# The last norm of all rows read before the last three experts' sums, their tokens' rows summed and written apart

## The chip, the cores and the metric

The kernel runs on one core of a Trainium2 chip. What counts is the time of one execution on the device in microseconds (us). A core has five engines, each with an instruction queue of its own that it works off in order: TensorE (PE, with its weight loads as PEld), VectorE (DVE), ScalarE (ACT), GpSimd (POOL) and SyncE (SP). SyncE only issues transfers here; GpSimd issues the indirect ones, which gather or scatter rows by a list of row numbers. HBM is the chip's main memory, SBUF the core's working memory of 128 partitions, PSUM the memory that TensorE writes its sums to.

## The reference

One decoder layer over 2048 tokens of 1024 numbers: a mixer of attention and a gated recurrence, then a mixture of 32 experts, of which each token takes two, then a last norm. Only the end bears on the change:

```python
x = x + mixed @ w_out[layer]
h2 = rmsnorm(x, norm2_g[layer])
x = x + hier_moe(h2, ...)      # each token: two experts, silu(h @ w_gate) * (h @ w_up) @ w_down, times a gate
...
return rmsnorm(x, norm_f_g)    # x * rsqrt(mean(x * x) + 1e-6) * g, row by row
```

A row of the output depends on that row's sum alone: the residual x and the two experts' rows of the token. Most rows are therefore complete before the last expert has run.

## The kernel before

The layer ends in `phase_c` (L1567), a loop over 32 experts sorted by their number of tokens; each has a fixed capacity of rows (`CAPS`: 192 down to 128). `even_order` (L101) decides in which order they run: the first is fixed, the others are mixed so that large and small ones alternate, and the last two are held back for the end. The experts are called E0 to E31 here, by their place in that order. The last ones have these capacities: E26 188, E27 128, E28 128, E29 192, E30 128, E31 128. A large expert (over 128) takes TensorE longer in each stage, and its result has to be transposed back and is scattered in two pieces, of 128 rows and of the rest.

For each expert there is a gather of its tokens' rows of h2 (`expert_in`, L1679, GpSimd), transposes (`expert_x`), the products with gate and up weights (`expert_up`), the hidden transposes of a small expert (`expert_hid`, L1756), the down product (`expert_down`, L1767) and the scatter of the result, which adds the rows onto the tensor x2d in HBM (`expert_out`, L1806, an accumulating indirect transfer on GpSimd). Each scatter into x2d waits for the landing of the one before, since both may touch one row. TensorE's program order is written out by hand: up of E(r), then down of E(r-1), and so on; the last is up of E30, down of E29, down of E30, up of E31, down of E31. The result transposes of a large expert E(r) stand in the up stage of E(r+2), or, for E29, in the down stage of E30. Weights come through SyncE: eight pieces of 0.5 MB for gate and up, four for down (`weights_down`, L1673, tile eD, eight buffers, so the four of an expert wait until the expert two places ahead has used its own).

The end, before the change, is this. While E31's up stage runs, nothing else is moved but the last scatters. Once E30's rows are scattered into x2d, `expert_base` (L1834) gathers E31's token rows from x2d into a tile, and `final` (L1851) loads all 16 tiles of 128 rows of x2d, forms each row's sum of squares on ScalarE (L1843), the reciprocal root in seven small steps of ScalarE and VectorE (`rsqrt`, L182), multiplies on VectorE (L1849) and stores the tile into the output. E31's down product is never added to x2d: VectorE adds it to the gathered rows (L1794), these are normed the same way, and when all 16 stores have landed one indirect scatter writes them over the output's rows (L1811). A list entry that is no token has a row number beyond the output and is skipped there. After that, `overflow` (L1420) runs only if an expert had more tokens than its capacity.

SyncE's transfers to and from one tensor and buffer are held apart by semaphores, and each transfer on SyncE waits for the one eight places ahead of it to have landed.

## Time and profile before

| | us |
|---|---|
| median of 3 runs | 2217.72 (2206.78 to 2219.48) |
| the profiled execution | 2217.23 |
| its span | 2215.3 |
| TensorE busy | 1967.0 (89%) |
| VectorE busy | 1493.8 (67%) |
| ScalarE busy | 1201.4 (54%) |
| GpSimd busy | 567.3 (26%) |
| transfers of SyncE's queue, share of 16 engines | 56.7% |
| transfers of GpSimd's queue, share of 16 engines | 8.5% |

The profile is of one execution, taken by the hardware. The span runs from its first to its last instruction, and all points of time below are counted from its start. "Busy" adds up an engine's instructions; an average over stages with different limits says little on the end, so the rows further down are of the last 160 us. A wait is put down to what ended it last.

### The profile page before, as it was taken

What the parts mean: (1) busy time and instruction counts of PE and PEld (TensorE: products, weight loads), DVE (VectorE), ACT (ScalarE), POOL (GpSimd) and SP (SyncE); (2) the same over time, 40 slices, a digit from 0 to 9 for tenths busy, and PEclk for the clock granted to TensorE, in tenths of its full rate; (3) what the DMA queues carried; (4) which work ended last, traced back from release to release, by engine and by line L of the source; (5) the groups of instructions that cost most, each with busy time, mean ns of one, the idle gap of its engine ahead of it and who ended that gap; (6) DMA issues with size and microseconds to landing.
All of it is one profiled execution on the core that took longest, in us unless ns stands there. A gap on an engine that the chain in (4) does not pass through costs nothing. (4 is left out here: it accounts for less than half of the span.)

```text
span 2215.3 us, 39749 instructions
## 1 busy us (share of the span) xinstructions
PE 1967.0 (89%) x13753; PEld 1345.8 (61%) x13777; DVE 1493.8 (67%) x4121; ACT 1201.4 (54%) x2646; POOL 567.3 (26%) x620
## 2 busy tenths in 40 slices
PE   4998978999899998899888998699999999999981
PEld 4645565555655556455444445569999977766750
DVE  6657787767857777567887677756656656556525
ACT  6455653765547655566554343456556655555524
POOL 2303244123431335411431112212233222111110
PEclk9998988998999998999899998799999999999995
DMA  7333254532535324553578995799999999999857
GB/s 229 85 94 96 66 128 112 114 90 70 118 101 123 83 75 113 174 119 71 128 168 226 290 253 164 253 353 315 312 311 314 329 315 313 325 325 321 302 149 299
DMA packets 438896, 433.37 MB, mean 196 GB/s; under 512 B 242644, under 2 KB 325716, under 8 KB 438176
## 3 DMA queue, kind: packets, MB, share of 16 engines
q1 hardware_dynamic: 420464, 382.74, 56.7%
q0 software_dynamic: 14064, 46.46, 8.5%
q8 instruction: 109, 1.79, 0.3%
q10 hardware_dynamic: 4160, 1.58, 0.3%
q14 instruction: 99, 0.81, 0.1%
HBM read 305.30 MB, written 66.29 MB: 168 GB/s over the span
## 5 line engine op out<-in xcount | busy, mean ns | idle before, releaser
L1660 DVE TENSOR_TENSOR eL<-eraw,eH 128x1024 bf16<-128x1024 f32 x248 | 298.0, 1218 | 107.9 <-ACT eH L1654 97.0
L1654 ACT ACTIVATE eH<-eraw 128x1024 fp32r<-128x1024 f32 x252 | 258.4, 1053 | 123.8 <-PE acc L1745 48.8
L453 ACT ACTIVATE P<-S,orow,fqk 128x256 f32<-128x256 f32 (+1 forms) x384 | 195.0, 512 | 172.3 <-DVE orow L447 94.1
L567 PE MATMUL proj<-whh,x 128*128 128x512 f16 x512 | 202.4, 395 | 0.1
L568 PE MATMUL proj<-whl,x 128*128 128x512 f16 x512 | 200.1, 391 | 0.0
L569 PE MATMUL proj<-whh,x 128*128 128x512 f16 x512 | 199.5, 390 | 0.0
L1726 PE MATMUL acc<-xs,eH 128*128 128x352 f32 (+15 forms) x1216 | 195.2, 313 | 1.8 <-DVE xs L1704 1.8
L436 PE MATMUL S<-k,qs 128*128 128x256 f16 (+1 forms) x768 | 172.4, 355 | 13.9 <-ACT P L453 10.9
L1726 PEld LDWEIGHTS acc<-xs,eH 128*128 128x128 f32 x1216 | 176.2, 190 | 4.7 <-issue 2.2
L440 DVE CUSTOM_DVE_ANT_0 S<-S,bias 128x256 f32<-128x256 f32 (+1 forms) x384 | 141.4, 369 | 54.8 <-PE S L436 51.6
L456 DVE TENSOR_TENSOR Ps<-P,Ps 128x256 f16<-128x256 f32 (+1 forms) x192 | 129.7, 675 | 68.8 <-ACT Ps L455 67.2
L1828 POOL DMA_INDIRECT x2d<-yo,sidx x49 | 105.2, 2146 | 255.7 <-DVE yo L1803 95.8
L1776 PE MATMUL acc<-hs,eD 128*128 128x176 f32 (+15 forms) x1216 | 165.1, 295 | 4.9 <-DVE ts L1751 3.0
L1776 PEld LDWEIGHTS acc<-hs,eD 128*128 128x128 f32 x1216 | 161.1, 190 | 6.0 <-DVE ts L1751 3.9
L1687 POOL DMA_INDIRECT xg<-h2d,gidx x49 | 56.1, 1146 | 334.0 <-PE tr L1701 159.6
L436 PEld LDWEIGHTS <-qs 128*128 128x128 f16 x768 | 89.5, 123 | 69.3 <-issue 20.3
L260 POOL TENSOR_TENSOR wraw<-wraw,g 128x1024 f32<-128x1024 f32 x44 | 84.7, 1928 | 167.8 <-DMA wraw<-in_w_in_dram 134.5
L1744 PE MATMUL acc<-eH,xs 128*128 128x512 f32 x208 | 118.4, 569 | 0.0
L1788 PE MATMUL acc<-eD,hs 128*128 128x512 f32 x208 | 98.0, 609 | 21.2 <-ACT yo L1801 11.5
L386 PE MATMUL proj<-wh,x 128*128 128x128 f16 x512 | 96.5, 231 | 18.9 <-DVE V L394 18.9
L455 ACT ACTIVATE Ps<-P 128x256 f16<-128x256 f32 (+1 forms) x192 | 102.8, 536 | 7.6 <-DMA PT<-Ps 5.0
L658 POOL TENSOR_SCALAR sw<-Sp,hw 128x128 f32<-128x128 f32 x112 | 53.3, 476 | 196.5 <-DVE Sp L661 106.5
(396 smaller groups left out, 4891.6 us busy)
## 6 DMA issues: line engine op xcount, KB each, us to landing
eraw<-in_w_gate_dram SPq DMA_DIRECT2D x128, 512.0 KB, 7.1
eD<-in_w_down_dram SPq DMA_DIRECT2D x128, 512.0 KB, 6.4
eraw<-in_w_up_dram SPq DMA_DIRECT2D x124, 512.0 KB, 6.3
wraw<-in_w_in_dram SPq DMA_DIRECT2D x41, 512.0 KB, 4.1
od<-orow SPq DMA_DIRECT2D x64, 132.0 KB, 2.0
R<-od SPq DMA_DIRECT2D x64, 132.0 KB, 2.4
xt<-in_x_dram SPq DMA_DIRECT2D x16, 512.0 KB, 4.8
wraw<-in_w_out_dram SPq DMA_DIRECT2D x16, 512.0 KB, 4.1
```

Of the source, the lines that this page charges most:

```text
L436: nc.tensor.matmul(ps[:, h, :W], q, self.block_cols(D['k'][h][:, x], br, blk, True), start=(x == 0), stop=(x == 1))
L440: nc.vector.tensor_tensor_reduce(ps[:, h, :W], ps[:, h, :W], bias[:, 256 - W:256], 1.0, -3.0e38, OP.add, OP.max, mx[:, h:h + 1])
L453: nc.scalar.activation(P[:, h], ps[:, h, :W], AF.Exp, bias=nm[:, h:h + 1], scale=f[:, h:h + 1], accum_out=orow[:, 130 + h:131 + h])
L456: nc.vector.tensor_tensor(hv[:, 1], P, hv[:, 0], op=OP.subtract)
L567: nc.tensor.matmul(ps, self.XH[n // 4][:, k, ns], W['whh'][:, k, :], start=(k == 0), stop=False)
L568: nc.tensor.matmul(ps, self.XH[n // 4][:, k, ns], W['whl'][:, k, :], start=False, stop=False)
L569: nc.tensor.matmul(ps, self.XL[n // 4][:, k, ns], W['whh'][:, k, :], start=False, stop=(k == KT - 1))
L1654: nc.scalar.activation(H, raw, AF.Copy)
L1660: (nc.gpsimd if on_pool else nc.vector).tensor_sub(L, raw, H.bitcast(F32))
L1726: nc.tensor.matmul(gu[:, i, 0:2 * cap], w[:, o:o + 128], xs[:, k], start=(k == 0), stop=False, skip_group_check=True)
L1744: nc.tensor.matmul(gu[:, j], xs[:, k, 0], H[:, fs], start=(k == 0), stop=False)
L1776: nc.tensor.matmul(py[:, j, 0:cap], W['w_down', f][:, o:o + 128], hs[:, f], start=(f == 0), stop=(f == 3))
```

## The change

The order holds back three experts instead of two (`LATE`), so the 192 one becomes E28, and E29, E30 and E31 are all of capacity 128. The last norm of all rows starts from x2d as it is when E28's rows are in it, while E30's down stage and E31's stages run. The rows of E29, E30 and E31 no longer go into x2d. Instead `late_base` gathers the token rows of the three from x2d and writes them into the tensor mix (whose old content is no longer needed); E29's and E30's results are added onto mix by accumulating scatters; `late_rows` gathers the three experts' rows from mix; E31's result is added to its own tile of these on VectorE, as before. `late_out` norms the three tiles and scatters them into the output, one after the other, behind all stores. `final` is split into loads, norms and stores of some tiles (`final_load`, `final_norm`, `final_store`), with one chain of small steps for a group of tiles instead of one for each; the tiles lie in the buffers eraw, eH and eD. The rest of the diff are the overflow code's bounds.

```diff
-NB = NE + 1
+NB = NE + LATE            # LATE = 3
@@ even_order
-    last = left[-2:]
-    left = left[:-2]
+    last = left[-LATE:]
+    left = left[:-LATE]
@@ phase_c
+                    if r == NE - 2:
+
+                        self.late_base()
+                        self.final_load(0, RAW)
+                        self.weights_down(E[r + 1])
+                        self.final_load(RAW, 9)
                     if r == NE - 1:
-                        self.expert_base(E[r])
-                        self.final()
+                        for e in (E[r], E[r - 1], E[r - 2]):
+                            self.late_rows(e)
...
+                    if r == NE - 1:
+                        self.final_norm(RAW, 9)
+                        self.final_store(3, 9)
+                        self.final_load(13, NT)
                     if r >= NE - 2:
                         for _ in self.expert_down(E[r]):
                             next(out, None)
-                        out = chain(out, self.expert_out(E[r]))
+                        if r < NE - 1:
+                            out = chain(out, self.expert_out(E[r]))
+                    if r == NE - 2:
+                        self.final_norm(0, RAW)
+                        self.final_store(0, 3)
+                        self.final_load(9, 13)
...
-                    if r + 1 < NE:
+                    if r + 1 < NE - 1:
                         self.weights_down(E[r + 1])
-                for _ in out:
-                    pass
+                self.final_norm(9, 13)
+                self.final_store(9, 13)
+                self.final_norm(13, NT)
+                self.final_store(13, NT)
+                for e in E[-LATE:]:
+                    self.late_out(e)
@@ expert_out
-            nc.gpsimd.indirect_dma_start(out=self.x2, in_=yo, in_offset=None,
+            nc.gpsimd.indirect_dma_start(out=self.mix if late else self.x2, in_=yo, in_offset=None,
                                          out_offset=bass.IndirectOffsetOnAxis(ap=self.sidx[0:w, i, r:r + 1], axis=0),
-                                         compute_op=OP.add)
+                                         compute_op=OP.add, **(dict(bounds_check=S - 1, oob_is_err=False) if late else {}))
@@ new
+    def late_base(self):
+
+        nc = self.nc
+        self.exp_on = True
+        for E, nm in zip(self.E[-LATE:], ("xg0", "yo1", "yT")):
+            r = E['r']
+            x = self.mx.tile([128, DM], F32, name=nm)
+            nc.gpsimd.indirect_dma_start(out=x, out_offset=None, in_=self.x2[0:S],
+                                         in_offset=bass.IndirectOffsetOnAxis(ap=self.gidx[:, 0, r:r + 1], axis=0))
+            nc.gpsimd.indirect_dma_start(out=self.mix, in_=x, in_offset=None,
+                                         out_offset=bass.IndirectOffsetOnAxis(ap=self.sidx[:, 0, r:r + 1], axis=0),
+                                         bounds_check=S - 1, oob_is_err=False)
+
+    def late_rows(self, E):
+        nm = {id(e): nm for e, nm in zip(self.E[-LATE:], ("yo1", "yT", "xg0"))}[id(E)]
+        x = E['xo'] = self.mx.tile([128, DM], F32, name=nm)
+        self.nc.gpsimd.indirect_dma_start(out=x, out_offset=None, in_=self.mix,
                                           in_offset=bass.IndirectOffsetOnAxis(ap=self.gidx[:, 0, E['r']:E['r'] + 1], axis=0))
+    def late_out(self, E):
+
+        nc = self.nc
+        self.normed(E['xo'], self.fs, self.mw.tile([128, DM], BF16, name="eL", bufs=HS))
+        nc.gpsimd.indirect_dma_start(out=self.out, in_=E['xo'], in_offset=None,
+                                     out_offset=bass.IndirectOffsetOnAxis(ap=self.sidx[:, 0, E['r']:E['r'] + 1], axis=0),
+                                     bounds_check=S - 1, oob_is_err=False)
+    def final_norm(self, a, b):
+        nc, n = self.nc, b - a
         junk = self.mw.tile([128, DM], BF16, name="eL", bufs=HS)
+        ss = self.fs.tile([128, n], F32, name="gss")
+        for i in range(n):
+            nc.scalar.activation(junk, self.X[a + i], AF.Square, accum_out=ss[:, i:i + 1])
+        if a <= RAW:
+            self.exp_set()
+        rs = self.fs.tile([128, n], F32, name="grs")
+        self.rsqrt(rs, ss, n, 1.0 / DM, self.fs)
+        for i in range(n):
+            x = self.X[a + i]
+            nc.vector.scalar_tensor_tensor(x, x, rs[:, i:i + 1], self.gf, op0=OP.mult, op1=OP.mult)
```

GpSimd's queue at the end of the program, first before the change: the scatters of E28's rows (yo), of E29's in two pieces (yo) and of E30's (xg), the gather of E31's rows and their scatter into the output. A name behind the arrow is what is read, one ahead of it what is written.

```order
L1828 DMA x2d<-yo_24163,sidx 2304x1024
L1687 DMA xg_24415<-h2d,gidx 128x1024
L1828 DMA x2d<-yo_24417,sidx 2304x1024
L1828 DMA x2d<-yo_24617,sidx 2304x1024
L1828 DMA x2d<-yo_24636,sidx 2304x1024
L1828 DMA x2d<-xg_24613,sidx 2304x1024
L1837 DMA xg_24715<-x2d,gidx 128x1024
L1811 DMA out_dram<-xg_24715,sidx 2048x1024
```

And after the change, from E28's second piece on; three scatters into the output, of the tiles yo, yT and xg, follow the last row shown.

```order
L1842 DMA x2d<-yo_24593,sidx 2304x1024
L1855 DMA xg_24622<-x2d,gidx 128x1024
L1855 DMA yo_24627<-x2d,gidx 128x1024
L1855 DMA yT<-x2d,gidx 128x1024
L1857 DMA mix<-xg_24622,sidx 2048x1024
L1857 DMA mix<-yo_24627,sidx 2048x1024
L1857 DMA mix<-yT,sidx 2048x1024
L1842 DMA mix<-yo_24663,sidx 2048x1024
L1842 DMA mix<-xg_24681,sidx 2048x1024
L1864 DMA xg_24789<-mix,gidx 128x1024
L1864 DMA yT<-mix,gidx 128x1024
L1864 DMA yo_24793<-mix,gidx 128x1024
```

Behind E28's second piece there are now 14 transfers instead of, behind E30's, two; the three scatters into mix and the two accumulating ones stand in one line ahead of the gathers from mix.

SyncE's queue, before: the last down weights of E31 (eD), then the loads of the 16 tiles, then their stores.

```order
L1676 ISA
L1676 DMA eD<-in_w_down_dram 128x1024
L1861 DMA eraw<-x2d 128x1024 x6
L1861 DMA eH<-x2d 128x1024 x10
L1865 DMA out_dram<-eraw 128x1024 x6
L1865 DMA out_dram<-eH 128x1024 x10
```

And after; ahead of the first row shown stand the six loads eraw<-x2d and the first three of E31's four down weights.

```order
L1696 DMA eD<-in_w_down_dram 128x1024
L1896 DMA eH<-x2d 128x1024 x3
L1915 DMA out_dram<-eraw 128x1024 x3
L1896 DMA eD<-x2d 128x1024 x4
L1915 DMA out_dram<-eraw 128x1024 x3
L1915 DMA out_dram<-eH 128x1024 x3
L1896 DMA eraw<-x2d 128x1024 x3
L1915 DMA out_dram<-eD 128x1024 x4
L1915 DMA out_dram<-eraw 128x1024 x3
```

Loads and stores now alternate, and E31's down weights stand between the sixth and the seventh load.

VectorE's queue near E31's down product, before: its two halves are added to the gathered rows (L1794, xg) between the small steps and multiplications of the first tiles (eraw).

```order
L191 TENSOR_TENSOR rs_t<-rs_y 128x1
L1794 SCALAR_TENSOR_TENSOR xg_24715<-acc,gate,xg_24715 128x512
L192 TENSOR_TENSOR rs_t<-rs_t,rs_v 128x1
L193 TENSOR_SCALAR rs_t<-rs_t 128x1
L187 TENSOR_SCALAR rs_v<-fss 128x1
L194 TENSOR_TENSOR frs<-rs_y,rs_t 128x1
L191 TENSOR_TENSOR rs_t<-rs_y 128x1
L1849 SCALAR_TENSOR_TENSOR eraw<-eraw,frs,gf 128x1024
```

And after: the first half (L1814) stands behind the multiplications of tiles 6 to 8 (eH) and ahead of the small steps and multiplications of tiles 9 to 12 (eD); those of tiles 13 to 15 and of the three late row tiles follow further down.

```order
L1911 SCALAR_TENSOR_TENSOR eH<-eH,grs,gf 128x1024 x3
L1814 SCALAR_TENSOR_TENSOR xg_24789<-acc,gate,xg_24789 128x512
L188 TENSOR_SCALAR rs_v<-gss 128x4
L192 TENSOR_TENSOR rs_t<-rs_y 128x4
L193 TENSOR_TENSOR rs_t<-rs_t,rs_v 128x4
L194 TENSOR_SCALAR rs_t<-rs_t 128x4
L195 TENSOR_TENSOR grs<-rs_y,rs_t 128x4
L1911 SCALAR_TENSOR_TENSOR eD<-eD,grs,gf 128x1024
L1814 SCALAR_TENSOR_TENSOR xg_24789<-acc,gate,xg_24789 128x512
L1911 SCALAR_TENSOR_TENSOR eD<-eD,grs,gf 128x1024 x3
```

What moved is the place of that add: seven of the 16 tiles' multiplications now stand behind it.

## Rows read from the trace of the kernel before

**Rows 1.** The page: its first line.

```profile
span 2215.3 us, 39749 instructions
```

**Rows 2.** SyncE's waits from 2120 to the end: us in total, times, longest.

```profile
SPq L1861 <- DMA x2d<-xg,sidx: 23.2, 1, 23.2
```

**Rows 3.** SyncE's issues in order of time: start, us, engine, line, what.

```profile
2155.44 3.02 SPq L1861 DMA_DIRECT2D eraw<-x2d  x6
...
2180.16 13.20 SPq L1865 DMA_DIRECT2D out_dram<-eH  x10
```

**Rows 4.** Stretches: length, busy PE, PEld, DVE, ACT, POOL, clock, DMA share, GB/s.

```profile
2120.00:2125.00 5.00, 4.93 (x32) 4.97 (x32) 0.69 (x1) 1.09 (x2) 0.00 (x0) 1.00 0.00 0
...
2160.00:2165.00 5.00, 3.04 (x4) 1.49 (x5) 1.95 (x7) 4.79 (x10) 0.00 (x0) 0.50 1.01 402
2185.00:2190.00 5.00, 0.00 (x0) 0.00 (x0) 5.00 (x18) 3.08 (x14) 0.00 (x0) 0.50 1.03 419
```

**Rows 5.** TensorE in order of time: the first matmuls of its stages.

```profile
2059.53 0.52 PE L1744 MATMUL acc<-eH,xs 128*128 128x512 f32 x1
...
2074.24 3.60 PE L1788 MATMUL acc<-eD,hs 128*128 128x512 f32 x8
...
2082.37 2.82 PE L1726 MATMUL acc<-xs,eH 128*128 128x384 f32 x13
...
2100.14 3.63 PE L1788 MATMUL acc<-eD,hs 128*128 128x512 f32 x8
...
2107.68 0.80 PE L1744 MATMUL acc<-eH,xs 128*128 128x512 f32 x1
...
2120.07 5.20 PE L1776 MATMUL acc<-hs,eD 128*128 128x192 f32 x31
...
2130.91 1.88 PE L1788 MATMUL acc<-eD,hs 128*128 128x512 f32 x4
...
2161.96 5.38 PE L1788 MATMUL acc<-eD,hs 128*128 128x512 f32 x8 [8.49 <-ACT hs L1764]
```

**Rows 6.** GpSimd in order of time: indirect transfers, start and us of their issue.

```profile
2068.65 1.62 POOL L1828 DMA_INDIRECT x2d<-yo,sidx  x1 [0.30 <-issue]
2078.82 1.48 POOL L1828 DMA_INDIRECT x2d<-yo,sidx  x1 [8.55 <-ACT yo L1801]
2085.41 1.58 POOL L1828 DMA_INDIRECT x2d<-yo,sidx  x1 [5.12 <-issue]
...
2136.91 1.57 POOL L1828 DMA_INDIRECT x2d<-yo,sidx  x1 [25.95 <-DVE yo L1803]
2144.14 1.44 POOL L1828 DMA_INDIRECT x2d<-yo,sidx  x1 [5.66 <-DMA x2d<-yo,sidx]
2149.10 1.56 POOL L1828 DMA_INDIRECT x2d<-xg,sidx  x1 [3.52 <-DMA x2d<-yo,sidx]
...
2202.46 1.02 POOL L1811 DMA_INDIRECT out_dram<-xg,sidx  x1 [45.27 <-SPq L1424]
```

**Rows 7.** Transfers by line: count, median us from issue to landing.

```profile
xg<-x2d,gidx POOLq DMA_INDIRECT x1, 8.0
out_dram<-xg,sidx POOLq DMA_INDIRECT x1, 3.3
```

**Rows 8.** Accumulating scatters (L1828): us from issue to landing.

```profile
DMA to landing us min/median/max: 4.7/8.2/10.6
```

**Rows 9.** Gathers from h2d (L1687): us from issue to landing.

```profile
DMA to landing us min/median/max: 3.6/6.7/9.9
```

**Rows 10.** Groups from 2155: names, shapes, count, busy us, mean ns, idle before.

```profile
L1849 DVE SCALAR_TENSOR_TENSOR eH<-eH,frs,gf 128x1024 f32<-128x1024 f32 x10 | 12.4, 1279 | 0.0
L1843 ACT ACTIVATE eL<-eH 128x1024 bf16<-128x1024 f32 x10 | 10.5, 1048 | 2.8 <-ACT rs_y L189 1.3 <-ACT eL L1843 0.9 <-DVE rs_v L187 0.6
...
L187 DVE TENSOR_SCALAR rs_v<-fss 128x1 f32<-128x1 f32 x17 | 2.5, 146 | 10.2 <-ACT eL L1843 10.2
```

**Rows 11.** Transfers by queue, 2130 to 2155: packets, MB, share of 16 engines.

```profile
q0 software_dynamic: 367, 1.31, 36.4%
```

More of the change, by code (lines that the diff above doesn't have):

```diff
@@ L83 @@
 FIXED = 1
+LATE = 3
 PRE = 4
@@ L1425, in overflow @@
             with tc.tile_pool(name="ov", reuse_waits=RW, bufs=1) as t:
-                r = self.E[-1]['r']
-                nc.vector.memset(self.capr[:, r:r + 1], 0.0)
+                for E in self.E[-LATE:]:
+                    nc.vector.memset(self.capr[:, E['r']:E['r'] + 1], 0.0)
                 self.route_over()
@@ L1807, in expert_out @@
         nc, r, cap = self.nc, E['r'], E['cap']
-        if E is self.E[-1]:
-            x = E['xo']
-            self.normed(x, self.fs, self.mx.tile([128, DM], F32, name="xg1"))
-            nc.gpsimd.indirect_dma_start(out=self.out, in_=x, in_offset=None,
-                                         out_offset=bass.IndirectOffsetOnAxis(ap=self.sidx[:, 0, r:r + 1], axis=0),
-                                         bounds_check=S - 1, oob_is_err=False)
-            return
+        late = any(E is e for e in self.E[-LATE:])
         for i, w in E['tails']:
@@ L1827, in expert_out @@
                 yo = E['yo']
-            nc.gpsimd.indirect_dma_start(out=self.x2, in_=yo, in_offset=None,
+            nc.gpsimd.indirect_dma_start(out=self.mix if late else self.x2, in_=yo, in_offset=None,
                                          out_offset=bass.IndirectOffsetOnAxis(ap=self.sidx[0:w, i, r:r + 1], axis=0),
-                                         compute_op=OP.add)
+                                         compute_op=OP.add, **(dict(bounds_check=S - 1, oob_is_err=False) if late else {}))
             yield
-    def expert_base(self, E):
-        x = E['xo'] = self.mx.tile([128, DM], F32, name="xg0")
-        self.nc.gpsimd.indirect_dma_start(out=x, out_offset=None, in_=self.x2[0:S],
-                                          in_offset=bass.IndirectOffsetOnAxis(ap=self.gidx[:, 0, E['r']:E['r'] + 1], axis=0))
+    def late_base(self):
[13 more added lines that the diff above has]
+        self.nc.gpsimd.indirect_dma_start(out=x, out_offset=None, in_=self.mix,
+                                          in_offset=bass.IndirectOffsetOnAxis(ap=self.gidx[:, 0, E['r']:E['r'] + 1], axis=0))
+    def late_out(self, E):
[4 more added lines that the diff above has]
+                                     bounds_check=S - 1, oob_is_err=False)
     def normed(self, x, pool, junk):
@@ L1849, in normed, with final_load, final_store @@
         nc.vector.scalar_tensor_tensor(x, x, rs, self.gf, op0=OP.mult, op1=OP.mult)
-    def final(self):
-        nc = self.nc
-        self.exp_on = False
-        junk = self.mw.tile([128, DM], BF16, name="eL", bufs=HS)
-        X = []
-        for n in range(NT):
-            if n < RAW:
-                x = self.mraw.tile([128, DM], F32, name="eraw", bufs=RAW)
-            else:
-                x = self.mw.tile([128, DM], F32, name="eH", bufs=HS)
-            nc.sync.dma_start(x, self.x2[128 * n:128 * n + 128])
-            X.append(x)
-        for n, x in enumerate(X):
-            self.normed(x, self.fs, junk)
-            nc.sync.dma_start(self.out[128 * n:128 * n + 128], x)
+    def final_load(self, a, b):
+        if a == 0:
+            self.X = []
+        for n in range(a, b):
+            if n < RAW or n > 12:
+                x = self.mraw.tile([128, DM], F32, name="eraw", bufs=RAW)
+            elif n < 9:
+                x = self.mw.tile([128, DM], F32, name="eH", bufs=HS)
+            else:
+                x = self.mw.tile([128, DM], F32, name="eD", bufs=DS)
+            self.nc.sync.dma_start(x, self.x2[128 * n:128 * n + 128])
+            self.X.append(x)
+    def final_norm(self, a, b):
+        nc, n = self.nc, b - a
+        junk = self.mw.tile([128, DM], BF16, name="eL", bufs=HS)
+        ss = self.fs.tile([128, n], F32, name="gss")
[8 more added lines that the diff above has]
+            nc.vector.scalar_tensor_tensor(x, x, rs[:, i:i + 1], self.gf, op0=OP.mult, op1=OP.mult)
+    def final_store(self, a, b):
+        for n in range(a, b):
+            self.nc.sync.dma_start(self.out[128 * n:128 * n + 128], self.X[n])
     def run(self, ctx, out):
```

## The prediction

> **What bounds the kernel now.** I read the profile in five steps. First the span, 2215.3 us [rows 1]; the execution itself took 2217.23 us, 0.5 us under the median of the three runs (2217.72), so a difference of spans carries over to the median. Second, SyncE's waits in the last 96 us: one of 23.2 us, where the first load of the last norm waits for the last expert scatter into x2d that precedes it [rows 2]. Third, SyncE's issues: those loads start at 2155.44, and the last stores belong to a row that begins at 2180.16 and goes on for 13.2 us [rows 3]. Fourth, the 5-us stretches: at 2120 the transfers stand still (0 GB/s) while TensorE is full, and from 2160 the transfers are full (402 to 419 GB/s) while TensorE has almost nothing left [rows 4]. Last, GpSimd: it scatters E31's rows into the output at 2202.46, when all stores have landed [rows 6], and the span ends 2215.3 - 2202.46 - 3.3 = 9.5 us after that scatter landed [rows 1, 6, 7].
>
> So the tail is 32 transfers of 0.5 MB, bound by bandwidth: 0.524 MB at about 410 GB/s is 1.28 us, times 32 is 41 us, and 2155.4 + 1.5 + 41 + 1.3 (the one gather) is 2199, three us ahead of GpSimd's scatter.
>
> **The change, part by part.** Times are on the span of before.
>
> *When the loads can start.* The capacity-192 expert moves from E29 to E28, and the loads wait for E28's second scatter only. TensorE goes from stage to stage nearly without gaps here, so I lay its stages anew with their own lengths [rows 5]: E28 up before 14.7 us (2059.53 to 2074.24, with the transposes of a large expert's result in it), E27 down 8.1, E29 up 17.8 (large), E28 down 7.5, E30 up 12.4, E29 down 10.8 (large). The result transposes are worth 14.7 - 12.4 = 2.3. After: E28 up 17.8 + 2.3 to 2079.6; E27 down to 2087.7; E29 up 12.4 to 2100.1; E28 down 10.8 to 2110.9; E30 up 14.7 to 2125.6. E28's first scatter starts 9.1 us into E30's up stage, as E26's did (2068.65 against 2059.53) [rows 5, 6]: 2120.0. The next one waits for its landing, 7.2 us (2136.91 to 2144.14, quiet transfers): 2127.2. It lands as its like did, 4.96 us less 0.7 of restart (2144.14 to 2149.10): 2131.5. Under load the two steps were 10.2 and 6.6 (2068.65, 2078.82, 2085.41 [rows 6]), which gives 2136. I take 2131.5, since the order on SyncE leaves the queue empty there as it is now at 2120 [rows 4]. The loads start **24 us earlier**. This is the gain that the change offers.
>
> *What it adds on the transfers.* Six gathers of 0.52 MB, three plain scatters and two accumulating ones of roughly 100 rows, two more scatters into the output. E31's four down weights (0.52 MB each), which land ahead of the tail now, stand behind the first six loads. From 2131.5 to the last landed store: 36 transfers of 1.28 are 46.1; six gathers at 1.28 are 7.7; three plain scatters about 1.0 each; two accumulating ones about 2.7 each (estimate: queue 0 took 36.4% of 25 us for 320 rows, so 3.6 us for 128, times 95/128) [rows 4, 11]. Together 62 us, so 2195 with 1.5 of start: 4 us ahead of the 2199 of before. The bandwidth alone therefore eats 20 of the 24 us.
>
> Here the Trainium skill speaks against the change: "DMA: Bandwidth & Descriptors", section "Issuing engines are not separate DMA queues", says that transfers started by any engine run on the same 16 DMA engines and interleave. The share of queue 0 agrees [rows 11]. By that rule the 62 us stand as they are; if GpSimd's transfers had room of their own the last store would land at 2179 instead of 2195.
>
> *The new chain on GpSimd.* Its queue is in order, and each of these waits for the landing of the one ahead: gather from x2d, three scatters into mix, two accumulating scatters, then the gathers from mix. Landing times: accumulating 4.7 / 8.2 / 10.6 (least, median, most) [rows 8]; gather 3.6 / 6.7 / 9.9 [rows 9], and 8.0 in the full tail [rows 7]; a plain scatter is there once, 3.3 on quiet transfers [rows 7], 10.6 is its upper bound. Full transfers add 4.4 to a gather (8.0 against 3.6) and 1.9 to an accumulating scatter (8.2 against the 6.3 of 2149.10 to 2155.44 [rows 3, 6]); so I take 6.5 for the plain scatter, between 5.2 and 7.7, nearer the loaded rows because the transfers are full from 2133 on. With 0.7 of restart each: 7.4 + 3 x 7.2 + 2 x 8.9 + 6.7 (the last gather, transfers thinning, 6.0) = 53.5. So E31's row tile, with the other experts' sums in it, arrives at **2185**. With all steps at their least it is 2131.5 + 4.3 + 3 x 4.0 + 2 x 5.4 + 4.3 = 2163; with all at their most, 2131.5 + 10.6 + 5 x 11.3 + 10.6 = 2209.
>
> *What stands behind that gather.* VectorE adds E31's first half onto the gathered tile, in order, ahead of the roots and multiplications of tiles 9 to 12, of 13 to 15 and of the three late row tiles (the order in the section on the change). So seven of the 16 stores wait for it. Behind it: the add 0.75, TensorE's second half 5.4 at the low clock (0.50 granted after its idle time, the 1.2 GHz level) [rows 4, 5], in whose cover one root (about 2, seven steps of 0.15 to 0.2 each) and one multiplication of 1.28 lie [rows 10]; the second add 0.75; three multiplications 3.9; the next roots with one square between them 3.5; three multiplications 3.9. That is about 18.2; then the last store, issue and landing about 4: 22 us, so 2207. Then three scatters into the output, one behind the other, 0.75 + 3.3 each [rows 6, 7]: 12.2 instead of 4.1. Then the 9.5 us of the end: **2229**, 13.5 us behind the 2215.3 of before.
>
> *At nothing.* The squares and multiplications of tiles 0 to 8 (nine of each, 1.05 and 1.28 [rows 10]) lie beside the up stage of E31 and the chain; uncovered they would be 11 us on VectorE. Two more table loads on ScalarE and the stop of E30's down stage behind three squares end by 2160, 25 us ahead of the gather. The Python count NB and the overflow code run only for overflowing experts, which this execution has none of.
>
> **The sum.** 2217.23 + (2131.5 + 53.5 + 22 + 12.2 + 9.5 - 2215.3) = 2217.23 + 13.4 = 2230.6; I say 2230.
>
> **Rivals.**
> 1. *The transfers bind, not the chain* (2219 to 2221). If the chain's steps land near their least, the gather comes before 2173, and the last store is set by bandwidth: 2195 to 2197, + 12.2 + 9.5 = 2217 to 2219 on the span, 2 us more in the execution's time. For it: 320 rows of queue 0 in quiet time took 4.7 to 6.5 us each. Against it: those times were quiet, these are not. The skill's same page, section "Where 436 GB/s comes from", lets memory bind such transfers at about 358 GB/s; the rows show 402 to 419. By that rule this rival would give about 2227 (62 us times 410/358 in place of 62).
> 2. *The chain waits behind SyncE's queue* (2240 to 2255), the other side: slower. SyncE keeps up to eight transfers of 0.5 MB in flight (each waits for the one eight places ahead of it), and each GpSimd step shares the engines with them. At the loaded ends (scatters 10.6, gathers 9.9) the price is up to 24 us on top of 2185. It decides from a mean step of 9.0 us including restart, over the seven steps (I take 7.6): then the gather comes at 2194 and the whole is over 1% slower. For it: 10.2 us in the one loaded scatter [rows 6]. Against it: SyncE's stores pause for VectorE, so the queue is not eight deep throughout.
> 3. *The added traffic is free and the chain hidden* (2201). Then 24 us are won and 8.1 lost to the two more output scatters: 16 us faster, still within 1%. Against it: the 62 us of transfers above.
>
> **Chances.** My forecast (chain binds, 2223 to 2240) 0.52; rival 1, 0.20; rival 2, 0.20; rival 3 and better, 0.08. About 1% (22 us) is what a measurement of this kernel can tell from no change: its three runs lie 12.7 us apart. Over 1% faster needs 2195, which no sum here reaches: 0.04, half of rival 3. Over 1% slower is rival 2: 0.20. Within: 0.76. The range, 2214 to 2246, holds the forecast, rival 1 with some slack for the base, and the nearer half of rival 2.
>
> **What would show it.** Right: the first load of x2d near 2131; nine tiles normed by 2165; GpSimd's five scatters 6 to 10 us apart; VectorE idle for about 20 us in front of its add onto xg, released by the gather from mix; the transfers falling off before 2190; three output scatters 4 us apart. Wrong: a first load later than 2137, a gather from mix before 2173 or after 2194, or stores of tiles 9 to 12 ahead of it.

## The result

The changed kernel takes 2232.22 us (median of 9 runs, 2224.15 to 2237.9) beside 2214.24 us of the kernel before (9 runs, 2206.78 to 2223.55): a ratio of 1.0078, interval 1.0054 to 1.0102. It is 0.8% slower, inside the 1% that was forecast as most likely, and 2232 lies in the range and 2 us from the predicted 2230.

Two profiled executions of one kernel (8 and 9 below were profiled twice) are already 5 to 8 us apart near 1600 us, so points of the tail are told below from two marks within the same execution: **A**, the start of a gather of h2 near 1600 us on GpSimd (long before anything that was edited; after the change its row is the first of GpSimd's below), and **T**, the issue of the first load of x2d. A in the kernel before:

```profile
1599.34 0.91 POOL L1687 DMA_INDIRECT xg<-h2d,gidx  x1 [1.44 <-PE tr L1701]
```

| us | before | after |
|---|---|---|
| A | 1599.34 | 1599.53 |
| T, from A | 556.1 | 530.3 |
| end of the span, from T | 59.9 | 101.2 |
| end of the span, from A | 616.0 | 631.5 |

So the loads did start 25.8 us earlier, and the tail behind them became 41.3 us longer.

### The profile page after: what moved, and what is told of

Its sections match the earlier page's. It is cut to its first block, busy times and chain, and to the rows that moved or that the text cites. A ratio compares the mean times of both kernels' runs of the same rounds, so it can differ in the third digit from the quotient of the medians.

```text
span 2231.0 us, 39717 instructions
## 1 busy us (share of the span) xinstructions
PE 1971.9 (88%) x13777; PEld 1347.3 (60%) x13777; DVE 1491.1 (67%) x4073; ACT 1204.2 (54%) x2632; POOL 584.7 (26%) x630
## 5 line engine op out<-in xcount | busy, mean ns | idle before, releaser
L1842 POOL DMA_INDIRECT x2d<-yo,sidx x48 | 108.9, 2269 | 238.0 <-DVE yo L1823 53.8
L1707 POOL DMA_INDIRECT xg<-h2d,gidx x49 | 56.6, 1155 | 327.5 <-PE tr L1721 177.3
```

## The profile after

The page's first line:

```profile
span 2231.0 us, 39717 instructions
```

SyncE's issues in order of time (start, us, engine, line, what):

```profile
2129.80 2.87 SPq L1896 DMA_DIRECT2D eraw<-x2d  x6
...
2162.75 2.73 SPq L1915 DMA_DIRECT2D out_dram<-eH  x3
2165.53 2.09 SPq L1896 DMA_DIRECT2D eraw<-x2d  x3
2190.47 8.12 SPq L1915 DMA_DIRECT2D out_dram<-eD  x4
2201.94 2.72 SPq L1915 DMA_DIRECT2D out_dram<-eraw  x3
```

The loads start at 2129.80 instead of 2155.44 [rows 3]. Between 2168 and 2190 SyncE issues nothing; before, it went on storing until 2193 [rows 3]. SyncE's waits from 2120 on (us in total, times, longest) put that pause down to VectorE, whose norms the stores of tiles 9 to 12 (eD) need:

```profile
SPq L1915 <- DVE eD L1911: 27.6, 3, 21.9
```

VectorE in turn waits for GpSimd, whose order of time is this (start and us of the issue; in brackets the idle time ahead and what ended it):

```profile
1599.53 0.92 POOL L1707 DMA_INDIRECT xg<-h2d,gidx  x1 [1.42 <-PE tr L1721]
...
2130.55 1.00 POOL L1855 DMA_INDIRECT xg<-x2d,gidx  x1 [4.08 <-PE acc L1808]
...
2138.97 1.02 POOL L1857 DMA_INDIRECT mix<-xg,sidx  x1 [4.89 <-DMA xg<-x2d,gidx]
2148.24 1.01 POOL L1857 DMA_INDIRECT mix<-yo,sidx  x1 [8.25 <-DMA mix<-xg,sidx]
2156.33 0.98 POOL L1857 DMA_INDIRECT mix<-yT,sidx  x1 [7.08 <-DMA mix<-yo,sidx]
2164.50 2.07 POOL L1842 DMA_INDIRECT mix<-yo,sidx  x1 [7.19 <-DVE eH L1911]
2175.50 1.56 POOL L1842 DMA_INDIRECT mix<-xg,sidx  x1 [8.93 <-DMA mix<-yo,sidx]
2182.41 1.00 POOL L1864 DMA_INDIRECT xg<-mix,gidx  x1 [5.35 <-DMA mix<-xg,sidx]
...
2208.85 1.01 POOL L1871 DMA_INDIRECT out_dram<-yo,sidx  x1 [22.93 <-SPq L1425]
2212.91 1.01 POOL L1871 DMA_INDIRECT out_dram<-yT,sidx  x1 [3.04 <-DMA out_dram<-yo,sidx]
2216.92 0.98 POOL L1871 DMA_INDIRECT out_dram<-xg,sidx  x1 [3.00 <-DMA out_dram<-yT,sidx]
```

Six steps in a row (three gathers at once, five scatters), each behind the landing of the one ahead, take 51.9 us from the first gather to the gather from mix. One of these waits, ahead of 2164.50, is put down to VectorE; the same step in experiment 3 is put down to the landing of the scatter ahead of it. VectorE (same columns):

```profile
2161.44 3.68 DVE L1911 SCALAR_TENSOR_TENSOR eH<-eH,grs,gf 128x1024 f32<-128x1024 f32 x3
2187.02 0.75 DVE L1814 SCALAR_TENSOR_TENSOR xg<-acc,gate,xg 128x512 f32<-128x512 f32 x1 [21.91 <-issue]
...
2193.89 0.75 DVE L1814 SCALAR_TENSOR_TENSOR xg<-acc,gate,xg 128x512 f32<-128x512 f32 x1 [3.45 <-PE acc L1808]
2194.56 3.67 DVE L1911 SCALAR_TENSOR_TENSOR eD<-eD,grs,gf 128x1024 f32<-128x1024 f32 x3
```

Nine tiles are normed by 2165.1; then VectorE stands for 21.9 us in front of E31's add onto the gathered rows, and the norms of tiles 9 to 15 stand behind it. The row of that add names no releaser ("issue"). TensorE's rows rule out TensorE, since E31's first half is done by 2167.0 and the second half waits for the add:

```profile
2161.44 5.57 PE L1808 MATMUL acc<-eD,hs 128*128 128x512 f32 x8 [0.69 <-ACT hs L1784]
2187.83 6.03 PE L1808 MATMUL acc<-eD,hs 128*128 128x512 f32 x8 [20.82 <-DVE xg L1814]
```

What the add still lacks then is its gathered tile, whose gather is issued at 2182.41; experiment 2 brings that gather forward, and the wait goes.

Stretches of 25 us, and two of 5 us (length, busy PE, PEld, DVE, ACT, POOL, clock, DMA share, GB/s), show the transfers full and then nearly idle:

```profile
2130.00:2155.00 25.00, 21.27 (x68) 10.32 (x66) 8.29 (x12) 11.74 (x21) 4.94 (x5) 0.93 0.98 378
2155.00:2180.00 25.00, 6.68 (x12) 2.91 (x12) 6.70 (x11) 9.80 (x16) 4.61 (x3) 0.70 1.00 370
2180.00:2205.00 25.00, 6.03 (x8) 2.38 (x8) 12.44 (x27) 7.80 (x22) 2.91 (x3) 0.57 0.52 189
2205.00:2231.00 26.00, 0.00 (x0) 0.00 (x0) 3.66 (x11) 0.00 (x0) 2.99 (x3) 0.50 0.19 73
...
2170.00:2175.00 5.00, 0.00 (x0) 0.00 (x0) 0.00 (x0) 0.00 (x0) 0.00 (x0) 0.71 1.05 334
...
2180.00:2185.00 5.00, 0.00 (x0) 0.00 (x0) 0.00 (x0) 0.00 (x0) 1.98 (x3) 0.50 0.30 61
```

Before, the transfers stood still at 2120 and ran at 397 to 419 GB/s in every stretch of 5 us from 2160 to 2195, to the end of the stores (402 and 419 in the two of [rows 4]); now they are full 25 us earlier and at half from 2180 on, with seven of the 16 stores still to come.

## The experiments

Kernels are named by their edit against the changed one. "From T" is the profiled span's end less the first load's issue (after: 101.2). The intervals are of 95%; one that holds 1 shows no difference from the kernel before. Two profiles of one kernel (8 and 9) differ by 0.5 to 0.8 us from T and by up to 2.7 from A.

| edit | ratio to before, interval | end from T | end from A, less before's |
|---|---|---|---|
| the change itself | 1.0078, 1.0054 to 1.0102 | 101.2 | +15.5 |
| 1 norms of tiles 9 to 15 first | 1.0045, 1.0024 to 1.0066 | 95.3 | +9.8 |
| 2 base copy left out | 1.0007, 0.9991 to 1.0022 | 83.4 | -2.6 |
| 3 the 16 tiles left out | 0.9955, 0.9935 to 0.9976 | - | -13.3 |
| 4 four small experts last | 1.0066, 1.0043 to 1.0089 | 103.9 | +9.9 |
| 5 base kept apart | 1.0011, 0.9992 to 1.0029 | 87.0 | +1.5 |
| 6 base apart, four last | 1.0021, 1.0005 to 1.0036 | 95.5 | +6.1 |
| 7 as 5, other buffers | 0.9987, 0.9971 to 1.0004 | 78.8 | -5.4 |
| 8 as 7, four last | 0.9967 (0.9950 to 0.9985), again 0.9923 (0.9898 to 0.9949) | 79.9, 79.4 | -12.4, -12.2 |
| 9 as 8, late adds last | 0.9945 (0.9926 to 0.9964), again 0.9940 (0.9917 to 0.9963) | 80.5, 79.8 | -10.5, -7.9 |

**1. The norms of tiles 9 to 15 ahead of E31's add.** Does the wait in VectorE's queue cost what it looks like? The four calls move from the end of the program to here, and the late norms are queued behind them as the add is.

```diff
+                        self.final_norm(9, 13)
+                        self.final_store(9, 13)
+                        self.final_norm(13, NT)
+                        self.final_store(13, NT)
                     if r >= NE - 2:
                         for _ in self.expert_down(E[r]):
...
-                nc.vector.scalar_tensor_tensor(x, py, self.gate[:, 0, r:r + 1], x, op0=OP.mult, op1=OP.add)
+                with self.tc.issue_after(self.normed_last):
+                    nc.vector.scalar_tensor_tensor(x, py, self.gate[:, 0, r:r + 1], x, op0=OP.mult, op1=OP.add)
```

> One edit of the changed kernel: on VectorE and ScalarE the norms of tiles 9 to 15 stand ahead of E31's add onto xg and ahead of the three late norms; PE, GpSimd and SyncE keep their order. In the changed kernel the first of these adds waits 21.9 us for the gather from mix and seven norms, and SyncE's seven stores behind them, wait with it. Theory A (GpSimd's chain sets when the gather arrives, at 2187, and the stores queue behind VectorE's add): the last seven stores leave by about 2183, the three out scatters need only the late norms and start near 2191 in place of 2208.9; span about 2213, so -18 us against the changed kernel (2214 us, range 2209 to 2221, and the chain a little slower because the stores now share the engines with it). Rival B (the bytes bind, not the queue): the same 25 MB are to be moved from 2130 on, so the end moves by less than 4 us, 2228 or more.

It gave 7 us by the ratios (0.0033 of 2215, with overlapping intervals) and 6 in the profile (95.3 instead of 101.2 from T), not 18. SyncE's last issue in that kernel:

```profile
2187.86 2.72 SPq L1920 DMA_DIRECT2D out_dram<-eraw  x3
```

And GpSimd there, its last gather from mix and the first late scatter:

```profile
2192.66 0.94 POOL L1869 DMA_INDIRECT yo<-mix,gidx  x1 [0.31 <-issue]
2205.86 1.80 POOL L1876 DMA_INDIRECT out_dram<-yo,sidx  x1 [12.26 <-DVE yo L1889]
```

The stores did leave: the last ones are issued 53.8 us behind T (2187.86 - 2134.07) instead of 72.1. But the late rows arrive later: their last gather is squared 66.2 us behind T (in the changed kernel 60.9), because the stores that moved forward now share the engines with the chain (the step behind its last accumulating scatter takes 10.1 us instead of 6.9); with 5.6 us of norm the first late scatter comes at 71.8 instead of 79.1. Of that difference, 7.3, the profile's end keeps 5.9, since the late scatters follow each other 4.9 and 4.6 us apart there instead of 4.1 and 4.0. So the wait was real, but two ends lay close together: behind the stores stands the chain itself. My expectation counted the one and not the other; the rival, that bytes alone bind (under 4 us), does not fit the profile's 6 either.

**2. No base copy.**

```diff
     def late_base(self):
...
-            nc.gpsimd.indirect_dma_start(out=x, out_offset=None, in_=self.x2[0:S],
...
-            nc.gpsimd.indirect_dma_start(out=self.mix, in_=x, in_offset=None,
...
```

> One edit of the changed kernel: late_base's three gathers from x2d and three plain scatters into mix are left out, so the late experts' tokens get a wrong final row (their base is missing; mix still holds what stood there). All else stays. Theory A (a serialized chain of GpSimd transfers sets the end): the steps of 8.4 + 25.5 us go, the chain then starts with E29's rows (ready near 2131) and E30's (ready near 2144), the gather from mix arrives near 2163 instead of 2187, VectorE's add waits for PE (2167) and not for the gather, the last stores land near 2187 and the span is about 2210, -21 us (range 2204 to 2216). Rival B (the bytes bind): 3.1 MB fewer of 25 MB, so about -7 us, 2224. Rival C (the chain's adds, held by E30's rows and not by the base copy, decide): gather not before 2175, end about 2220.

The end comes 17.8 us earlier from T, level with the kernel before: theory A, somewhat less than its 21, and far from the 7 that fewer bytes would give. The gather from mix is issued at 2152.67, 25.5 us behind T instead of 52.6, so VectorE finds it there and waits 1.2 us for TensorE instead of 21.9:

```profile
2162.41 0.75 DVE L1814 SCALAR_TENSOR_TENSOR xg<-acc,gate,xg 128x512 f32<-128x512 f32 x1 [1.16 <-PE acc L1808]
```

What binds then shows in this kernel's stretches (columns as above):

```profile
2170.00:2175.00 5.00, 0.00 (x0) 0.00 (x0) 2.48 (x3) 1.59 (x3) 0.00 (x0) 0.53 1.03 420
2175.00:2180.00 5.00, 0.00 (x0) 0.00 (x0) 0.22 (x2) 4.77 (x11) 0.00 (x0) 0.50 0.81 331
2180.00:2185.00 5.00, 0.00 (x0) 0.00 (x0) 4.59 (x14) 1.04 (x8) 0.00 (x0) 0.50 0.35 138
```

The transfers are full until 2175; what follows are the last three tiles, whose loads waited for buffers, on their way through ScalarE and VectorE.

**3. The chain with SyncE's queue empty.**

All calls of `final_load`, `final_norm` and `final_store` are gone, as these three:

```diff
-                        self.final_load(0, RAW)
...
-                        self.final_norm(0, RAW)
-                        self.final_store(0, 3)
```

> The changed kernel without the last norm of the sixteen tiles: their 16 loads from x2d, squares, norms and 16 stores are left out (only the three late lists' rows are written to the output, the others are missing). What is left from 2130 on is the chain of GpSimd alone with E31's weights. It measures the chain's steps with SyncE's queue empty. Theory A1 (each step's length is stretched by the traffic of SyncE's queue): gather about 4, plain scatters about 4 each, adds about 6.5 each, gather 4; the gather from mix arrives near 2163 in place of 2187, E31's add is then bound by PE, end about 2193. Theory A2 (the steps are a fixed delay of a GpSimd transfer of 128 rows): steps stay near 8.4, 9.3, 8.1, 8.2, 11, 7, the gather arrives near 2184, end about 2215.

GpSimd of that kernel, as above:

```profile
2131.03 1.00 POOL L1845 DMA_INDIRECT xg<-x2d,gidx  x1 [3.94 <-PE acc L1798]
...
2139.21 1.02 POOL L1847 DMA_INDIRECT mix<-xg,sidx  x1 [4.67 <-DMA xg<-x2d,gidx]
2144.15 1.00 POOL L1847 DMA_INDIRECT mix<-yo,sidx  x1 [3.92 <-DMA mix<-xg,sidx]
2148.13 0.97 POOL L1847 DMA_INDIRECT mix<-yT,sidx  x1 [2.98 <-DMA mix<-yo,sidx]
2152.08 1.58 POOL L1832 DMA_INDIRECT mix<-yo,sidx  x1 [2.97 <-DMA mix<-yT,sidx]
2159.17 1.56 POOL L1832 DMA_INDIRECT mix<-xg,sidx  x1 [5.51 <-DMA mix<-yo,sidx]
2165.98 1.00 POOL L1854 DMA_INDIRECT xg<-mix,gidx  x1 [5.25 <-DMA mix<-xg,sidx]
```

The steps of the plain scatters, from issue to the next issue, take 4.9, 4.0 and 4.0 us instead of 9.3, 8.1 and 8.2, the accumulating ones 7.1 and 6.8 instead of 11.0 and 6.9; only the first gather, beside which E31's 2.1 MB of weights are loaded, stays at 8.2. From gather to gather it is 35.0 us instead of 51.9. So 17 us of the chain are the price of sharing the engines (theory A1), and the steps are no fixed delay. The end I expected (2193) was too early by 10.5 (2203.5): the gather from mix is issued at 2165.98 and not near 2159, the first late scatter follows it by 13.1 us (2179.12), and the late scatters stand 5.0 and 4.7 apart instead of 4.1. The run says more than the theory asked: with all 16 tiles gone the kernel is only 0.45% faster than before. The chain and what hangs on it alone nearly fill the time of the old tail.

**4. Four small experts last.** The 192 expert becomes E27.

```diff
-    last = left[-LATE:]
-    left = left[:-LATE]
+    last = left[-4:]
+    left = left[:-4]
```

> One number of the changed kernel's order: four experts of 128 rows stand last instead of three, so the expert of 192 rows that was E28 is E27, and E28 is a 128-row one with one scatter instead of two. x2d is then complete after one scatter of E28 that starts near 2107 to 2112 instead of 2125. Theory A (everything behind follows the start of the loads and of the base copy): loads start near 2118 instead of 2129.8, the whole tail moves by 9 to 12 us, span about 2220. Rival B (the end is bound by E31's matmuls and their norms, or by bytes of weights still under way at 2120): less than 4 us, 2227 or more.

The loads start 8.3 us earlier (522.0 from A instead of 530.3), the end comes 5.6 earlier in the profile and 2.7 by the ratios, whose intervals overlap (four runs), so a gain is not shown by them. By the ratios the rival's number holds, with another reason than it gave. In this kernel the gather that the first scatter into mix needs is issued third, at 2124.72, with six loads ahead of it, and the first step takes 14.3 us (2121.64 to 2135.95) instead of 8.4; the five others together take 40.9 instead of 43.4. So the gather from mix comes 5.6 us earlier from A, and the end as much.

**5. The base kept apart.** The copy is taken off the chain instead of left out: `late_zero` scatters zeros onto E30's and E31's rows of mix long before, the gathered base stays in its tile (xo), and what is gathered from mix (mr) is added to it. E31's result goes onto its base, so VectorE's add no longer stands behind the gather from mix, and E29's rows, the first into mix, are written plainly instead of accumulated. The output is complete.

```diff
+                    if r == NE - 9:
+                        self.late_zero()
...
-                                         compute_op=OP.add, **(dict(bounds_check=S - 1, oob_is_err=False) if late else {}))
+                                         **(dict(bounds_check=S - 1, oob_is_err=False) if late else {}),
+                                         **({} if E is self.E[-LATE] else dict(compute_op=OP.add)))
...
     def late_base(self):
...
-            x = self.mx.tile([128, DM], F32, name=nm)
+            x = E['xo'] = self.mx.tile([128, DM], F32, name=nm)
...
-            nc.gpsimd.indirect_dma_start(out=self.mix, in_=x, in_offset=None,
...
     def late_out(self, E):
...
+        with self.tc.issue_after(self.hold_late):
+            nc.vector.tensor_add(E['xo'], E['xo'], E['mr'])
```

> The changed kernel with the base copy taken out of the chain instead of left out: the three gathers from x2d stay in their tiles (no scatter of them into mix); the rows of mix of E30's and E31's lists are set to zero by two plain scatters some ten experts earlier, E29's rows are written into mix plainly, E30's are accumulated, the three lists are gathered from mix into eH tiles and added by VectorE to the kept base rows, behind the norms of tiles 9 to 12. The result is complete. The run that left the base copy out ended at 2214.7 us, level with the kernel before. Theory A' (the chain through mix set the end, and once it is gone the bytes between 2130 and 2180 bind, with 23 us of three late scatters and the close behind the last store): as with the base left out, less the plain write (about 3 us off the chain, which no longer binds), 2212 us (2208 to 2217). Rival (GpSimd's chain still decides through E30's add and the gather): 2220 or more. Rival (the removed chain gives more than the run without a base copy showed): under 2207.

1.0011 beside 1.0007 with the copy left out: the price can be had back in a complete kernel, 15 us by the ratios and 14 in the profile, and that makes it level with the kernel before, not faster. Bytes do not explain this: the three gathers of the base are still there, and the three plain scatters that are gone, about 1.0 us of transfers each in the prediction's sum, are 3 us together (an estimate). How much of the 15 is the shorter chain, and how much the add that no longer waits for it, is not separated. From its first gather to the gather from mix the chain takes 28.0 us (2132.32 to 2160.32) instead of 51.9. The expected 2212 lay 2.7 us under the kernel before as measured until then; measured was 2.5 above it (2220.7 beside 2218.2 in the same runs), so the expectation was 5 us too good.

**6. The same with four small experts last.** The diff is that of 4, and the norms of tiles 0 to 5 stand behind E30's gating.

> The version with the base kept apart, and four experts of 128 rows at the end as in the run on the order, which brought the loads 8 us forward but the end only 3.6 us, since the chain was held by E29's and E30's rows and by traffic; the norms of tiles 0 to 5 stand behind E30's gating so that they don't hold it. Theory A' (bytes bind from the start of the loads): loads start near 2121, the last store lands about 6 us earlier than without this order, end 2206 (2201 to 2212). Rival (the norms, not the bytes, are now last: E31's matmuls end at the same time in both): within 3 us of the version without the order.

A miss: no gain (2221.4 beside 2220.7 of kernel 5, where 2206 was expected). Its first stores are issued 36.0 us behind T (2167.99 - 2131.98) instead of 21.8 (2153.40 - 2131.57 in kernel 5), since ScalarE took the squares of two groups of tiles in turn and the roots of both began only at 2163.1, behind the last of these squares. ScalarE also changed its function tables nine times from 2125 on instead of three as in kernel 5, 1.28 us each. Two stretches of this kernel show the transfers idling meanwhile:

```profile
2160.00:2165.00 5.00, 1.64 (x8) 0.74 (x6) 0.24 (x2) 4.93 (x9) 1.09 (x2) 0.95 0.53 187
2165.00:2170.00 5.00, 0.18 (x1) 0.18 (x2) 4.14 (x12) 4.94 (x11) 1.80 (x2) 0.50 0.84 267
```

With two things changed at once it says nothing on the order of the experts; that the order of the norms undid its gain is read from this trace and not tested by itself.

**7 and 8. Other buffers in the tail, then four small experts last.** E31's down weights go to eraw, ahead of the loads of x2d; tiles 0 and 1 to eraw, 2 to 4 to eH, 5 to 12 to eD, 13 to 15 to eH; and each group of norms is queued behind the one before, the first behind E30's gating; the stores follow in the order of the tiles. All edits of 5 are in it too.

```diff
     def weights_down(self, E):
+            if E is self.E[-1]:
+                w = E['W']['w_down', h] = self.mraw.tile([128, 1024], F32, name="eraw", bufs=RAW)
...
     def final_norm(self, a, b):
+            for k in self.hold_norm if a else ():
+                st.enter_context(self.tc.issue_after(k))
```

> The version with the base kept apart (level with the kernel before) with other buffers in the tail: E31's down weights go to four eraw buffers that are free near 2115, ahead of SyncE's wait for x2d, so their 2.1 MB move while the engines are at 100 to 250 GB/s; tiles 5 to 12 are loaded into E29's and E30's eD buffers, tiles 13 to 15 into eH buffers that E31's gate and up matmuls leave, so that no load waits for a store; the norms stand in order of tiles behind E30's gating. Theory A' (bytes bind from x2d's completion to the last store, then 23 us of three late scatters and the close): 2.1 MB less at 415 GB/s is 5 us, and the 9 us in which the engines were at 116 to 318 GB/s ahead of the last three stores shrink to 3 or less; together 9 to 11 us under the version with the base kept apart (2220.7 beside 2218.2 of before), 2208 to 2212 in that call's terms, ratio 0.995 to 0.997. Rival (VectorE's and ScalarE's norms bind, not bytes): ratio 1.000 or more.

> The same with four experts of 128 rows at the end. Loads start 8 to 9 us earlier relative to E31's work; as long as buffers free in time (E29's and E30's eD buffers free no earlier than before) the engines start 5 tiles and 3 gathers 8 us earlier. Theory A' (bytes bind): 4 to 7 us less than without the order, ratio 0.992 to 0.995. Rival (buffers and E30's and E31's work set the tail): the same as without the order, within 2 us.

7 gave 5 us over 5 (0.9987 beside 1.0011; 7 to 8 in the profiles) where 9 to 11 were expected. 8 gave 4 more (4 to 7 expected) and is 0.3 to 0.8% faster than the kernel before, clear of the intervals; its ratio, 0.9967, missed the expected 0.992 to 0.995 in the first set of runs and met it in the second (0.9923). In 8 the end from T is that of 7, and the gain is that T comes 7 to 8 us earlier from A. Three stretches of 8 (its second profile):

```profile
2130.00:2155.00 25.00, 23.40 (x77) 11.29 (x76) 7.79 (x13) 15.08 (x25) 3.93 (x4) 1.00 1.03 388
2155.00:2180.00 25.00, 11.62 (x25) 4.88 (x24) 21.25 (x36) 16.48 (x34) 3.95 (x3) 0.79 0.99 394
2180.00:2205.00 25.00, 0.00 (x0) 0.00 (x0) 5.29 (x16) 0.41 (x2) 3.41 (x3) 0.50 0.24 94
```

And GpSimd there, the first late scatter:

```profile
2184.85 1.43 POOL L1887 DMA_INDIRECT out_dram<-xg,sidx  x1 [24.42 <-SPq L1425]
```

Now the transfers are full for 50 us and nearly done, where in the changed kernel 189 GB/s dragged on to 2205.

**9. The late adds behind the norms of tiles 13 to 15.** In 8 these adds stand ahead of those norms, and the last stores are issued at T + 50.2 (2178.09 - 2127.90).

> The version with the other buffers and four 128-row experts last, with VectorE's three adds of mix rows and the late norms' instructions on VectorE placed behind the norms of tiles 13 to 15. Before, these adds (1.2 us each) and waits of their squares stood ahead of those norms, so that the last three stores were issued at 2172.9 although their tiles were squared by 2162.5, while the engines moved 322 and 216 GB/s in 2170 to 2180. Theory A' (the last store's landing starts the three late scatters and the close): the last three stores are issued near 2169, 3 to 4 us earlier, the end 2 to 4 us earlier, ratio 0.995 (0.993 to 0.9965). Rival (the late rows' own add, square and norm, which end at 2180 in the version before, are as late as the stores and then decide): the first late scatter moves by less than 1 us, ratio as before, 0.9967.

> The version with other buffers and four 128-row experts last, once more, beside the version whose late adds stand behind the norms of tiles 13 to 15, on one chip and in turn, since their ratios (0.9967 and 0.9945) came from two calls and their intervals overlap, and since counted from the first load the first late scatter came at 57.5 us in the one and 57.9 us in the other. If the stores decide: this one is 2 to 4 us behind. If the late rows' own path decides as soon as the stores are out of the way: the two agree within 1.5 us.

> The version with the late adds behind the norms of tiles 13 to 15, beside the one with them ahead. If the stores decide: 2 to 4 us ahead of it, ratio near 0.9945 again. If the late rows' own path takes over: within 1.5 us of it.

The last stores did go 3.5 us earlier (T + 46.7), but the first late scatter stayed: T + 56.6 instead of 57.0. GpSimd's row of 9 (second profile) names VectorE as its releaser, that of 8 above SyncE:

```profile
2187.34 1.65 POOL L1887 DMA_INDIRECT out_dram<-xg,sidx  x1 [24.46 <-DVE rs_t L192]
```

Side by side the ratios are 0.9923 and 0.9940 with overlapping intervals; the medians, 2200.7 and 2203.4, stand 2.7 us apart the wrong way for a gain. The late rows' own path takes over at once, as the rival had it, and no gain of this edit is shown.

## Why the prediction was right, point by point

It named five terms; this is what they measured, on the span of after.

| term, us | predicted | measured |
|---|---|---|
| first load of x2d | 2131.5 | 2129.8 |
| GpSimd's chain, until the gather from mix has landed (taken as VectorE's add, 2187.02) | 53.5 | 57.2 |
| from there to the first late scatter | 22 | 21.8 (2208.85) |
| three late scatters | 12.2 | 11.3 (2216.92 + 3.2) |
| end behind them | 9.5 | 10.9 |
| end of the span | 2228.7 | 2231.0 |

- *The start of the loads.* Right to 1.7 us: the stages laid anew by their own lengths gave it.
- *The chain.* The mechanism was right and its length 7% short. The first gather took 8.4 (7.4 said), the plain scatters 9.3, 8.1 and 8.2 (7.2 each), the accumulating ones 11.0 and 6.9 (8.9 each), the last gather 4.6 (6.7). The mis-sized term is the plain scatter: I placed its landing at 6.5 between a quiet 3.3 and a bound of 10.6, and by the steps less 0.7 of restart the three measured 8.6, 7.4 and 7.5 (the trace gives 7.3 for one). That is 3.9 us over three steps; the first gather adds 1.0 and its later start 0.8, and the last gather gives 2.1 back. In experiment 3, without SyncE's loads and stores, the same scatters land in 4.2, 3.2 and 3.2.
- *What would show it.* It came: the first load at 2129.8 (2131 said), nine tiles by 2165.1 (2165), VectorE idle for 21.9 us (20; the row names no releaser, and the gather was told from TensorE's rows and experiment 2), the transfers falling off from 2170 (before 2190), the late scatters 4.0 us apart; of the five scatters' steps one, 11.0, lies outside the 6 to 10.
- *What stands behind the gather.* Right, and for the reason given: seven norms and stores behind VectorE's add. Experiment 1 adds what the prediction did not see, that with the stores out of the way the late rows' own path is only 7 us shorter.
- *Bandwidth.* That the bytes alone eat most of the earlier start was an estimate; the sum by it (the first rival) gave 2219 to 2221 against 2217.2, a ratio of 1.001 to 1.002. Experiments 2 and 5, where the chain is shorter and VectorE does not wait for it, measured 1.0007 and 1.0011. That this agrees is in part luck: experiment 2 moves about 3.1 MB less than the sum counts, and in it the transfers are full only until 2175, with the last three stores still to be issued at 2182.5. The other price that the prediction names for this rival, about 2227, is off by 1 to 3 us: its factor of 410/358 on the 62 us gives 2228 to 2230.
- *The rivals.* The first, that transfers bind, fell: they drop to 334 GB/s at 2170 and to 61 at 2180. The second, that SyncE's queue stretches the chain, has the right mechanism: 17 us of the 52 are of that kind. They were already in the loaded rows that the sum used, so its price on top was small; it decided at a mean step of 9.0 us and the mean was 8.2. The third, a hidden chain, fell by experiment 2: the copy alone costs 16 (by the ratios) to 18 us (from T).
- *The difference.* 13.4 us over the profiled execution were predicted. The spans differ by 15.7, the medians by 18.0; 2.3 of that are the terms above, whose errors of 0.2 to 3.7 us partly cancel. The other 2.3 are no more than the spread of executions: the median of the kernel before lay between 2211.6 and 2218.2 from one set of runs to another. So a hit to 2 us is partly luck; what was forecast right is the way, the size to 5 us in 18, and the path. The 1% that the prediction gave as the least that can be told from no change was too wide: the 0.8% here stands clear of its interval.

Two rules of the Trainium skill, page "DMA: Bandwidth & Descriptors", can be set beside the runs. Its section "Anatomy of one DMA — SWDGE (gpsimd) path" gives a transfer of GpSimd about 2 us of fixed cost, mostly the receipt of the last write, plus its bytes at 436 GB/s; for a list's 128 rows, 0.52 MB, an estimate from it is 3.2 us. The traces agree on nearly empty engines (3.2 us from issue to landing for two plain scatters of experiment 3 and for the late scatters of the changed kernel), and not on loaded ones: 7.3 us in the changed kernel. The same page of the Trainium skill, in its section "Issuing engines are not separate DMA queues", says that transfers of all engines interleave on the same 16 DMA engines. Experiment 3 agrees, with 35.0 us against 51.9 for one chain.

## What to carry to other kernels

Work that is started early through a chain of dependent indirect transfers is paid for by the step, and each step by the traffic beside it: count the steps at the loaded price before moving such a chain under full transfers, and take off it whatever can be prepared earlier (zeros) or kept in a tile (the base). When a queue's wait is removed, look first for the path that ends next: here it was 7 us behind, and later less than 1. And look whether the order of buffers and norms keeps the transfers full: an earlier start of the loads came with no gain in kernel 6 and with 4 us in kernel 8, where that order is another.

## What the runs showed of the hardware

- A plain indirect scatter of one list lands in 3.2 us on nearly empty engines (experiment 3 and the late scatters) and in 7.3 to 8.6 beside SyncE's loads and stores (the changed kernel); an accumulating one in 6.1 to 6.3 (experiment 3) and, at full transfers, in 10.3 (the changed kernel, whose second one, where transfers thin out, took 6.2).
- One core's 16 DMA engines moved 388 and 394 GB/s over two whole stretches of 25 us, gathers and scatters among them (kernel 8, second profile), and 414 to 420 in single stretches of 5 us (the changed kernel, 2145 to 2170).
